# Four column blocks with the sums of B as the stationary side, in a Strassen-like matmul with a row logsumexp

## The chip, the cores and the metric

The kernel runs on one core of a Trainium2 chip. The metric is device time in microseconds (us), the median of several runs. TensorE multiplies a stationary tile of 128x128 (loaded by a weight load) with a moving tile of up to 512 columns and adds the result up in PSUM, which has eight banks of 128x512 f32. VectorE and ScalarE work on 128 rows at a time, GpSimd issues most of the loads, SyncE a few. Each engine works its own queue in order; semaphores tie the queues together.

## The reference

```python
m, k, n = 1024, 4096, 4096
a = randn(m, k); b = randn(k, n)        # float32
x = np.matmul(a, b)
out = logsumexp(x, axis=-1)             # 1024 values
```

The output is one number per row of a: the logarithm of the sum of exponentials over the 4096 columns of that row of the product.

## The kernel before, in words

The products are formed in float16 with float32 sums. A row tile m (there are 8) has 128 rows of a, interleaved: partition p of tile m is row 8p + m. A column block nb (there are 8) has 512 columns of b. The depth of 4096 is 32 slices of 128, taken in 16 pairs.

Apart from block 0 against the first six row tiles, which are plain matmuls (line 227), everything is computed in quarters, in the manner of Winograd's form of Strassen's scheme. A quarter q is two row tiles (2q and 2q+1) against one column block. It is cut in two along rows (the two tiles), depth (the two slices of a pair) and columns (halves of 256), so that four products of halves, c11, c12, c21, c22, are wanted. Instead of eight half-size products there are seven, m1 to m7, on sums of A's halves (s1, s2, s5, and two sums that are put in place in aT) and on sums of B's halves (T1, T4, T6 in the tile tb, and t3 and t7, put in place in the raw block). In the kernel before, A's sums are the stationary side (128x128) and B's sums are the moving side (256 columns). One product is 16 matmuls; a quarter is 112; a block of four quarters is 448. Line 413 issues them all. The order in a quarter is m1 into c11, m5 into c12, m2 into c21, m6 into c22, then m3 on top of c12, m4 on top of c21, m7 on top of c11. In between, ScalarE copies c11 and c12 out after m5 (line 484) and c21 after m2 (line 488), and c12 and c21 again after m3 and m4 (lines 561, 563). m3 writes into c12 only after the copy of line 484, and m7 into c11 likewise. VectorE puts the parts together (lines 498 to 573), takes the maximum of each row (line 89) into a column of the table negmax, and ScalarE takes the exponentials with that maximum as a bias and adds them up into the table tsum (line 94). Those exponentials are put off to the next quarter (the list pending), ahead of which stand that quarter's first copies.

The steps are listed in plan: step 0 is block 1 against quarters 0 to 2, steps 1 to 6 are blocks 2 to 7 against all four quarters, and the last two steps make up block 0 and block 1 against quarter 3. While a block is multiplied, GpSimd loads the next one (line 143) into the eight raw buffers, as soon as those of the block before it are free, and VectorE makes the next block's B sums in the last quarter of a block (the calls of make for t1, t6, t3, t4 and t7 under tail). Each make goes over four groups of four pairs, one instruction of 128x1024 float16 for each group. In step 6, after quarter 1, GpSimd reloads block 1 into the part of aT that is no longer needed (line 595); this load waits for the matmuls of quarter 1.

The order on every engine is the order in which the program emits the instructions (a manual schedule). PSUM tiles go round the eight banks.

At the start, GpSimd builds the identity for the transposes of a (line 295, in masks.py), then issues its loads; VectorE fills zeros, negmax and tsum (lines 294, 296, 297). SyncE brings the first piece of a and of b (lines 308, 313). TensorE does some warm matmuls on zeros (line 291), then transposes pieces of a (line 209) and multiplies them with block 0.

The last quarter (final) merges all columns of negmax and tsum row by row: the smallest of the negated maxima, the exponentials of the differences, the weighted sum, the logarithm (lines 116 to 127 and 515 to 549).

Of the kernel before, what the change touches and what calls it, by code (L numbers as in the profile page):

```python
# [13 lines left out]
def kernel(  # L14
# [6 lines left out]
    nc = tc.nc  # L21
    P = 128
    FD = 512
    H = FD // 2
    f32 = mybir.dt.float32
    f16 = mybir.dt.float16
    AX = mybir.AxisListType
    ALU = mybir.AluOpType
    AF = mybir.ActivationFunctionType
# [4 lines left out]
    MT, KT, NB = M // P, K // P, N // FD  # L34
    MP, KP = MT // 2, KT // 2
    G = 4
    GI = KP // G
# [5 lines left out]
    cst_pool = ctx.enter_context(tc.tile_pool(name="cst", bufs=1))  # L43
    bt_pool = ctx.enter_context(tc.tile_pool(name="btp", bufs=2 * G))
    fix_pool = ctx.enter_context(tc.tile_pool(name="fix", bufs=1))
# [3 lines left out]
    psum_pool = ctx.enter_context(  # L49
        tc.tile_pool(name="psum", bufs=8, space=bass.MemoryType.PSUM)  # L50
    )
# [6 lines left out]
            name=nc.get_next_instruction_name(),  # L58
# [7 lines left out]
    aT = cst_pool.tile([P, KP, 2, MP, 2, P], f16, name="aT")  # L66
    s1 = cst_pool.tile([P, KP, MP, P], f16, name="s1")
    s2 = cst_pool.tile([P, KP, MP, P], f16, name="s2")
    s5 = cst_pool.tile([P, KP, MP, P], f16, name="s5")

    tb = cst_pool.tile([P, 3, KP, H], f16, name="tb")
    stg_slots = tb.rearrange("p t (i j) n -> p (t i) (j n)", j=4)
    NSLOT = 3 * KP // 4
    ident = cst_pool.tile([P, P], f16, name="ident")
    negmax = cst_pool.tile([P, MT, NB + 1], f32, name="negmax")
    tsum = cst_pool.tile([P, MT, NB + 1], f32, name="tsum")

# [4 lines left out]
    def add(o, x, y):  # L82
        nc.vector.tensor_tensor(out=o, in0=x, in1=y, op=ALU.add)  # L83

    def sub(o, x, y):
        nc.vector.tensor_tensor(out=o, in0=x, in1=y, op=ALU.subtract)  # L86
# [44 lines left out]
    class Block:  # L131


        def __init__(self, nb, raw=None, sums=None):
            self.nb = nb
            self.raw = raw or [
                bt_pool.tile([P, GI, 2, FD], f16, name=f"b_{nb}_{g}", tag="bt")
                for g in range(G)
            ]
            self.T1, self.T4, self.T6 = sums or (tb[:, 0], tb[:, 1], tb[:, 2])  # L140

        def load(self, lo, hi):
            nc.gpsimd.dma_start(  # L143
                out=self.raw[lo // GI][:, lo % GI : lo % GI + hi - lo],
                in_=b_rows[:, lo:hi, :, ts(self.nb, FD)],
            )
# [6 lines left out]
        def b(self, i, kp, h):  # L153
            return self.raw[i // GI][:, i % GI, kp, ts(h, H)]

        def make(self, what, lo=None, hi=None):
            if lo is None:
                for g in range(G):
                    self.make(what, g * GI, (g + 1) * GI)
                return  # L160
            u = self.raw[lo // GI][:, lo % GI : lo % GI + hi - lo]
            b11, b12 = u[:, :, 0, 0:H], u[:, :, 0, H:FD]
            b21, b22 = u[:, :, 1, 0:H], u[:, :, 1, H:FD]
            if what == "t1":
                add(self.T1[:, lo:hi], b11, b22)
            elif what == "t6":
                add(self.T6[:, lo:hi], b11, b12)
            elif what == "t4":
                sub(self.T4[:, lo:hi], b21, b11)
            elif what == "t7":  # L170
                add(b21, b21, b22)
            else:
                sub(b12, b12, b22)
# [21 lines left out]
    def load_a(k0, kn, m):  # L195
        slot = stg_slots[:, loads[0] % NSLOT, 0 : kn * P]
        loads[0] += 1
        nc.gpsimd.dma_start(out=slot, in_=a_m[m, :, k0 * P : (k0 + kn) * P])  # L198
        stg[k0, m] = slot
# [55 lines left out]
    arrivals = []  # L255
# [33 lines left out]
    def warm(n):  # L289
        for _ in range(n):  # L290
            nc.tensor.matmul(acc[2][1], zeros[:, 0:P], zeros[:, 0:FD], start=True, stop=True)  # L291

    zeros = s5[:, KP - 1].rearrange("p q c -> p (q c)")
    nc.vector.memset(zeros[:, 0:FD], 0.0)
    make_identity(nc, ident)
    nc.vector.memset(negmax, 3.0e38)
    nc.vector.memset(tsum, 0.0)
    warm(6)

    coming = list(arrivals)  # L300
# [16 lines left out]
    def load(k0, kn, what, x):  # L317
        if len(coming) >= len(arrivals) - 2:
            first(k0, kn, what, x)
        elif what == "a":  # L320
            load_a(k0, kn, x)
        else:
            blk0.load(k0 // 2, k0 // 2 + 1)

    back = []
    for n, (k0, kn, what, x) in enumerate(arrivals):
# [22 lines left out]
    deferred = []  # L349

    def flush():
        for f in pending:
            f()
        pending.clear()
# [5 lines left out]
    again0 = lambda: Block(0, sums=[wide(t[:, :, 0:2]) for t in (s1, s2, s5)])  # L360
    again1 = lambda: Block(1, raw=[wide(aT[:, ts(g, GI), :, 0:2]) for g in range(G)])
    plan = [(lambda: blk1, range(MP - 1))]
    plan += [(lambda nb=nb: Block(nb), range(MP)) for nb in range(2, NB)]
    plan += [(again0, [MP - 1]), (again1, [MP - 1])]

    blk, nxt = None, blk1
    for step, (_, qs) in enumerate(plan):
        blk, nxt = nxt, None
        nb = blk.nb
        more = step + 1 < len(plan)  # L370
        early = more and plan[step + 1][0] is again0
        if more:
            if plan[step + 1][0] is again1:
                nxt = last
            else:
                nxt = plan[step + 1][0]()
                if step == 1:
# [4 lines left out]
                        out=ident[0:1, 0:2], in_=aT[0:1, 0, 0, MP - 1, :, 0]  # L382
# [5 lines left out]
        if step == 0:  # L388

            KH = K // 2  # L390
            for h in range(2):
                a16 = dram_pool.tile([2, P, KH], f16, name=f"a16_{h}")
                for m in range(2):
                    nc.gpsimd.dma_start(out=a16[m], in_=a_m[MT - 2 + m, :, ts(h, KH)])
                for m in range(2):
                    nc.sync.dma_start_transpose(
                        aT[:, ts(h, KP // 2), :, MP - 1, m, :].rearrange("p i t c -> p (i t) c"),
                        a16[m],
                    )
        quads = {}  # L400
        for q in qs:

# [5 lines left out]
            c11, c12 = r0[:, 0:H], r0[:, H:FD]  # L408
            c21, c22 = r1[:, 0:H], r1[:, H:FD]

            def product(c, lhs, rhs, start=False, k=(0, KP)):
                for i in range(*k):
                    nc.tensor.matmul(  # L413
                        c,
                        lhs(i),
                        rhs(i),
                        start=(start and i == 0),
                        stop=(i == KP - 1),
                        skip_group_check=True,
                    )  # L420
# [6 lines left out]
            if final:  # L427
                c22 = psum_pool.tile([P, FD], f32, name="c22", tag="ps")[:, 0:H]


            s = fix_pool.tile([P, 4, H], f32, name=f"s_{step}_{q}", tag="s")
            x, e = s[:, 1::2], s[:, 0:2]
            if final:
                e = fix_pool.tile([P, 2, H], f32, name="e_last", tag="e")
            if joint and q > 0:
                e = e_next
# [78 lines left out]
            if final:  # L515
# [30 lines left out]
                    out=w, in_=w, func=AF.Exp, bias=n0, scale=-1.0, accum_out=l0  # L546
# [44 lines left out]
            if step == 1 and q == 1:  # L591
                a_sums_early(slice(0, KP // 2), MP - 1)
                a_sums_late(slice(0, KP // 2), MP - 1)
            if early and q == 1:
                last = again1().load_all()

    nc.sync.dma_start(out=out.rearrange("(p mt) -> p mt", mt=MT), in_=lg)
# [30 lines left out]
```

## Time and profile before

| What | Number |
|---|---|
| Median of 12 runs | 422.68 us (422.0 to 423.65) |
| Time of the profiled execution | 422.68 us |
| Its span, first to last instruction | 420.4 us |
| Mean granted TensorE clock | 0.999 |
| PE busy | 414.5 us (99%) |
| PE weight loads busy | 349.1 us (83%) |
| DVE (VectorE) busy | 259.0 us (62%), 575 instructions |
| ACT (ScalarE) busy | 109.7 us (26%) |
| POOL (GpSimd) busy | 73.2 us (17%) |
| Moved by DMA | 53.37 MB, mean 127 GB/s |

The profiled execution's own time is 2.3 us above its span, and equals the median of the runs. The busy shares are averages over stages that have different limits. TensorE is called PE, its weight loads PEld, VectorE is DVE, ScalarE ACT, GpSimd POOL and SyncE SP. A group is told by line, engine, operation and what it writes and reads; then come its count, busy time, the mean duration of one in nanoseconds, and the idle time before it with what ended it. In a timeline each line has start, duration, engine, line, operation, and how many instructions were merged into it.

### The profile page before, as it was taken

What the parts mean: (1) busy time and instruction counts of PE and PEld (TensorE: products, weight loads), DVE (VectorE), ACT (ScalarE), POOL (GpSimd) and SP (SyncE); (2) the same over time, 40 slices, a digit from 0 to 9 for tenths busy, and PEclk for the clock granted to TensorE, in tenths of its full rate; (3) what the DMA queues carried; (4) which work ended last, traced back from release to release, by engine and by line L of the source; (5) the groups of instructions that cost most, each with busy time, mean ns of one, the idle gap of its engine ahead of it and who ended that gap; (6) DMA issues with size and microseconds to landing.
All of it is one profiled execution on the core that took longest, in us unless ns stands there. A gap on an engine that the chain in (4) does not pass through costs nothing.

```text
span 420.4 us, 8526 instructions
## 1 busy us (share of the span) xinstructions
PE 414.5 (99%) x3643; PEld 349.1 (83%) x3643; DVE 259.0 (62%) x575; ACT 109.7 (26%) x279; POOL 73.2 (17%) x113
## 2 busy tenths in 40 slices
PE   8999999999999999999999999999999999999996
PEld 2555558888888888888888888888888888888885
DVE  2466687978647783257812694336832587299955
ACT  2222341142132222122222212222221222222124
POOL 7767753001010020003000030000200030020000
PEclk9999999999999999999999999999999999999999
DMA  9999999999999299102990079400990039899000
GB/s 178 204 202 201 202 205 207 207 207 215 189 191 194 48 177 207 18 2 36 207 160 2 2 114 208 82 2 2 179 207 15 2 51 207 144 182 207 14 2 1
DMA packets 57845, 53.37 MB, mean 127 GB/s; under 512 B 10192, under 2 KB 56912, under 8 KB 57808
## 3 DMA queue, kind: packets, MB, share of 16 engines
q0 software_dynamic: 48928, 49.95, 72.0%
q1 hardware_dynamic: 8880, 2.89, 4.1%
q8 instruction: 28, 0.46, 0.4%
q14 instruction: 9, 0.07, 0.0%
HBM read 100.66 MB, written 2.10 MB: 244 GB/s over the span
## 4 chain that ended last, share of the span: by engine, by line
PE 98%; DMA 1%; DVE 0%; ACT 0%; issue 0%; SPq 0%; ACTq 0%
PE acc L413 84%; PE acc L227 10%; PE tps L209 2%; DMA raw_b<-in_b_dram 1%; PE z L413 0%; PE c L413 0%; PE acc L291 0%; DVE aT L220 0%; DVE s L105 0%; ACT s L545 0%; DVE b L314 0%; SPq L308 0%; ACT lg L548 0%; DVE lg L86 0%; DVE nmmin L105 0%
## 5 line engine op out<-in xcount | busy, mean ns | idle before, releaser
L413 PEld LDWEIGHTS <-aT 128*128 128x128 f16 x1856 | 181.6, 98 | 21.1
L413 PEld LDWEIGHTS <-s 128*128 128x128 f16 x1392 | 136.2, 98 | 16.0
L413 PE MATMUL acc<-tb,aT 128*128 128x256 f16 x880 | 108.5, 273 | 0.0
L413 PE MATMUL acc<-b,aT 128*128 128x256 f16 x896 | 106.6, 273 | 0.0
L413 PE MATMUL acc<-b,s 128*128 128x256 f16 x896 | 105.8, 273 | 0.0
L143 POOL DMA_DIRECT2D b<-in_b_dram x51 | 41.1, 816 | 236.6 <-PE acc L413 222.5
L83 DVE TENSOR_TENSOR s<-s 128x256 f32<-128x256 f32 x26 | 11.0, 421 | 77.9 <-ACT s L488 77.9
L413 PE MATMUL acc<-tb,s 128*128 128x256 f16 x448 | 56.9, 273 | 0.0
L86 DVE TENSOR_TENSOR s<-s 128x512 f32<-128x512 f32 (+1 forms) x55 | 30.7, 559 | 38.9 <-ACT s L563 38.0
L484 ACT COPY s<-acc 128x512 f32<-128x512 f32 x26 | 15.2, 585 | 139.3 <-PE acc L413 139.3
L227 PE MATMUL acc<-b,aT 128*128 128x512 f16 x192 | 50.7, 389 | 0.6 <-DVE aT L220 0.4
L94 ACT ACTIVATE acc<-acc,negmax 128x512 f32<-128x512 f32 (+1 forms) x64 | 42.0, 656 | 3.5 <-DVE negmax L89 3.5
L89 DVE TENSOR_REDUCE negmax<-acc 128x1 f32<-128x512 f32 (+1 forms) x64 | 40.4, 671 | 0.6 <-ACT s L523 0.6
L83 DVE TENSOR_TENSOR tb<-b 128x1024 f16<-128x1024 f16 (+1 forms) x64 | 36.1, 616 | 3.5 <-DMA b<-in_b_dram 3.5
L488 ACT COPY s<-acc 128x256 f32<-128x256 f32 x29 | 10.8, 372 | 76.7 <-PE acc L413 72.8
L227 PEld LDWEIGHTS <-aT 128*128 128x128 f16 x192 | 16.8, 99 | 15.1 <-DVE aT L220 1.6
L198 POOL DMA_DIRECT2D tb<-in_a_dram x47 | 25.6, 548 | 5.9 <-issue 1.7
L83 DVE TENSOR_TENSOR acc<-acc,s 128x256 f32<-128x256 f32 x56 | 23.3, 431 | 4.8 <-PE acc L413 0.6
L209 PEld LDWEIGHTS <-tb 128*128 128x128 f16 x192 | 15.0, 100 | 12.5 <-DVE tb L309 1.0
L222 ACT COPY aT<-tps 128x512 f16<-128x512 f16 x24 | 14.0, 585 | 39.1 <-PE tps L209 39.1
L220 DVE COPY aT<-tps 128x512 f16<-128x512 f16 x24 | 10.2, 423 | 19.8 <-PE tps L209 19.8
L83 DVE TENSOR_TENSOR s<-aT 128x256 f16<-128x256 f16 (+1 forms) x78 | 20.2, 313 | 2.2 <-ACT aT L222 2.2
(63 smaller groups left out, 188.0 us busy)
## 6 DMA issues: line engine op xcount, KB each, us to landing
b<-in_b_dram POOLq DMA_DIRECT2D x28, 1024.0 KB, 17.1
tb<-in_a_dram POOLq DMA_DIRECT2D x47, 128.0 KB, 5.9
b<-in_b_dram POOLq DMA_DIRECT2D x8, 512.0 KB, 13.4
aT<-in_b_dram POOLq DMA_DIRECT2D x4, 1024.0 KB, 15.0
b<-in_b_dram POOLq DMA_DIRECT2D x15, 256.0 KB, 6.2
a<-in_a_dram POOLq DMA_DIRECT2D x4, 512.0 KB, 30.0
raw_b<-in_b_dram SPq DMA_DIRECT2D x1, 512.0 KB, 3.9
raw_a<-in_a_dram SPq DMA_DIRECT2D x1, 256.0 KB, 2.8
```

The costliest lines, as they stand in the source:

```text
L83: nc.vector.tensor_tensor(out=o, in0=x, in1=y, op=ALU.add)
L86: nc.vector.tensor_tensor(out=o, in0=x, in1=y, op=ALU.subtract)
L89: nc.vector.tensor_reduce(out=negmax[:, m, nb : nb + 1], in_=pt, axis=AX.X, op=ALU.max, negate=True)
L94: nc.scalar.activation(out=pt, in_=pt, func=AF.Exp, bias=negmax[:, m, nb : nb + 1], scale=scale, accum_out=tsum[:, m, nb : nb + 1],)
L143: nc.gpsimd.dma_start(out=self.raw[lo // GI][:, lo % GI : lo % GI + hi - lo], in_=b_rows[:, lo:hi, :, ts(self.nb, FD)],)
L198: nc.gpsimd.dma_start(out=slot, in_=a_m[m, :, k0 * P : (k0 + kn) * P])
L209: nc.tensor.matmul(pst[:, ts(j, P)], src[:, ts(j, P)], ident, is_transpose=True, start=(j == 0), stop=(j == kn - 1),)
L222: nc.scalar.copy(out=dst, in_=v)
L227: nc.tensor.matmul(pt, aT[:, i, kp, m // 2, m % 2, :], blk0.raw[i // GI][:, i % GI, kp, :], start=(done[m] == 0), stop=(done[m] == KT - 1),)
L413: nc.tensor.matmul(c, lhs(i), rhs(i), start=(start and i == 0), stop=(i == KP - 1), skip_group_check=True,)
L484: nc.scalar.copy(out=e, in_=halves(r0))
L488: nc.scalar.copy(out=s[:, 2], in_=c21)
```

## The change

There are two parts.

At the start, the identity is built behind GpSimd's first load instead of ahead of it, and the fills of negmax and tsum move from VectorE to GpSimd, behind about two dozen of its loads.

For column blocks 3 to 6, the sides of the matmul are exchanged. B's sums, 128 columns at a time, are the stationary side, and A's sums of all four quarters, 512 columns, are the moving side. A block is now two turns, nt = 0 and 1; a turn takes 128 columns of each of the two column halves against all 1024 rows, with seven products of 16 matmuls of 512 columns, and has four PSUM tiles of a whole bank each. What comes out is turned: the columns of x lie on the partitions, and the rows of x along the free axis. So each finished PSUM tile goes through VectorE's transpose of 32x32 blocks into a scratch (two slots in the upper half of T4, and the tile e), a maximum over each block of 32, a subtraction with that row broadcast, an exponential on ScalarE, and a sum over each block of 32. Small tables tnm (in the identity's space) and tts keep the negated maxima and the sums; merge_turned brings the three entries of each into one after every turn. In block 7, after quarter 1, spread_turned copies the tables into columns 3 to 6 of negmax and tsum, with 32 small copies on GpSimd, ahead of the reload of block 1. The copies out of PSUM that ScalarE makes in the other blocks are left to VectorE in a wide turn.

The B sums are made one turn ahead: in turn 0 those of the same block's turn 1, and in turn 1 those of the next block. When the next block is 7, which is not wide, they have the full width, and t4 and t7 are made half before c11 is put together and half after it.

```diff
-    ident = cst_pool.tile([P, P], f16, name="ident")
+    ident_space = cst_pool.tile([P, 3 * P // 2], f16, name="ident")
+    ident = ident_space[:, 0:P]
+    WN = P // 4
+    tnm = ident_space.bitcast(f32).rearrange("p (a c) -> p a c", c=WN)
+    tts = cst_pool.tile([P, 3, WN], f32, name="tts")
+    tmin = cst_pool.tile([P, WN], f32, name="tmin")
...
+            if self.wide:
+                b11, b12, b21, b22 = [t[:, :, ts(nt, P)] for t in (b11, b12, b21, b22)]
...
-    make_identity(nc, ident)
-    nc.vector.memset(negmax, 3.0e38)
-    nc.vector.memset(tsum, 0.0)
     warm(6)
...
+        if len(coming) == len(arrivals) - 3:
+            make_identity(nc, ident)
+        if len(coming) == len(arrivals) - 3 * MT:
+            nc.gpsimd.memset(negmax, 3.0e38)
+            nc.gpsimd.memset(tsum, 0.0)
...
+    WIDE = range(3, NB - 1)
+    slots = tb[:, 1, KP // 2 : KP].rearrange("p i n -> p (i n)").bitcast(f32)
+    slots = [slots[:, 0:FD], slots[:, FD : 2 * FD]]
...
+    def lse_turned(c, slot, h, r):
+        nm = tnm[:, 1 + h, ts(r, WN // 2)]
+        v = blocks32(slot)
+        nc.vector.transpose(out=slot, in_=c)
+        nc.vector.tensor_reduce(out=nm, in_=v, axis=AX.X, op=ALU.max, negate=True)
+        add(v, v, nm.unsqueeze(-1).broadcast_to((P, WN // 2, 32)))
+        nc.scalar.activation(out=slot, in_=slot, func=AF.Exp)
+        return lambda: nc.vector.tensor_reduce(
+            out=tts[:, 1 + h, ts(r, WN // 2)], in_=v, axis=AX.X, op=ALU.add
+        )
+    def merge_turned():
+        nc.vector.tensor_reduce(
+            out=tmin, in_=tnm.rearrange("p a c -> p c a"), axis=AX.X, op=ALU.min
+        )
+        sub(tnm, tnm, tmin.unsqueeze(1).broadcast_to((P, 3, WN)))
+        nc.scalar.activation(out=tnm, in_=tnm, func=AF.Exp, scale=-1.0)
+        nc.vector.tensor_mul(out=tts, in0=tts, in1=tnm)
+        add(tts[:, 0], tts[:, 0], tts[:, 1])
+        add(tts[:, 0], tts[:, 0], tts[:, 2])
+        nc.vector.tensor_copy(out=tnm[:, 0], in_=tmin)
...
+            cols = lambda i, kp, h: blk.b(i, kp, h)[:, ts(nt, P)]
+            product(c11, lambda i: blk.T1[:, i], lambda i: s1[:, i], start=True)
+            product(c12, lambda i: cols(i, 1, 1), lambda i: s5[:, i], start=True)
+            product(c21, lambda i: cols(i, 0, 0), lambda i: s2[:, i], start=True)
+            flush()
+            nc.vector.tensor_copy(out=s[:, 1], in_=c12)
+            add(s[:, 1], s[:, 1], c21)
+            sub(s[:, 0], s[:, 1], c11)
+            for f in deferred:
+                f()
+            deferred.clear()
+            mk("t1")
+            product(c22, lambda i: blk.T6[:, i], lambda i: aT[:, i, 0, :, 1], start=True, stop=True)
+            mk("t6")
+            mk("t3")
+            product(c12, lambda i: cols(i, 0, 1), lambda i: aT[:, i, 0, :, 0], stop=True)
+            sub(s[:, 0], c12, s[:, 0])
+            add(c22, c22, s[:, 0])
+            end12 = lse_turned(c12, slots[0], 1, 0)
+            end22 = lse_turned(c22, slots[1], 1, 1)
+            product(c21, lambda i: blk.T4[:, i], lambda i: aT[:, i, 1, :, 1], stop=True)
+            sub(s[:, 1], c21, s[:, 1])
+            end12()
+            end21 = lse_turned(c21, slots[0], 0, 1)
+            end22()
+            for what in ("t4", "t7"):
+                if last:
+                    for g in range(G // 2):
+                        mk(what, g * GI, (g + 1) * GI)
+                else:
+                    mk(what)
+            product(c11, lambda i: cols(i, 1, 0), lambda i: aT[:, i, 1, :, 0], stop=True)
+            add(c11, c11, s[:, 1])
+            e = fix_pool.tile([P, FD], f32, name=f"ew_{blk.nb}_{nt}", tag="e")
+            end11 = lse_turned(c11, e, 0, 0)
+            end21()
+            if last:
+                for what in ("t4", "t7"):
+                    for g in range(G // 2, G):
+                        mk(what, g * GI, (g + 1) * GI)
+            deferred.extend([end11, merge_turned])
...
+        if blk.wide:
+            wide_step(blk, nxt)
+            continue
+        if step == 1:
+            nc.gpsimd.memset(tnm, 3.0e38)
+            nc.gpsimd.memset(tts, 0.0)
...
             if early and q == 1:
+                spread_turned()
                 last = again1().load_all()
```

Here last (inside wide_step) is true in turn 1 of block 6, and mk makes the B sums of the next turn. The list deferred holds the sum and the merge that a turn leaves to the next one.

## The prediction

> **What bounds it now.** I read the page first: span and the chain that ended last.
>
> ```profile
> span 420.4 us, 8526 instructions
> PE 98%; DMA 1%; DVE 0%; ACT 0%; issue 0%; SPq 0%; ACTq 0%
> ```
>
> TensorE sets the end. The chain in order of time says how:
>
> ```profile
> 58.25 3.45 PE acc L227 x16
> 61.71 347.72 PE acc L413 x3184
> ```
>
> From 61.71 us on there is no gap: 3184 matmuls of 256 columns in 347.72 us, 109.2 ns each. The 16 of 512 columns before them take 215.6 ns each, less than two of 256 (218.4). A block is 448 of these, 48.93 us. So blocks 3 to 6 lie at 147.3 to 343.0 us, and block 7 follows.
>
> Next, how much VectorE does there: the table by stage, for block 6.
>
> ```profile
> 294.10:343.00 48.90, 48.90 (x450) 43.84 (x448) 26.11 (x49) 12.19 (x32) 3.79 (x6) 1.00 0.53 87
> ```
>
> The columns after the stretch are its length, then PE, PEld, DVE, ACT and POOL. VectorE (DVE) is busy 26.1 of 48.9 us. Prices come from the groups with shapes apart:
>
> ```profile
> L83 DVE TENSOR_TENSOR tb<-b 128x512 f16<-128x512 f16 x16 | 6.0, 417 | 2.8 <-DMA b<-in_b_dram 2.8
> L86 DVE TENSOR_TENSOR s<-s 128x512 f32<-128x512 f32 x28 | 19.3, 688 | 38.0 <-ACT s L563 38.0
> L484 ACT COPY s<-acc 128x512 f32<-128x512 f32 x26 | 15.2, 585 | 139.3 <-PE acc L413 139.3
> ```
>
> and, since instructions overlap, from starts in VectorE's timeline:
>
> ```profile
> 184.49 1.28 DVE L89 TENSOR_REDUCE negmax<-acc 128x1 f32<-128x512 f32 x2
> 185.68 2.48 DVE L83 TENSOR_TENSOR tb<-b 128x1024 f16<-128x1024 f16 x4
> 191.53 0.43 DVE L83 TENSOR_TENSOR s<-s 128x256 f32<-128x256 f32 x1 [3.37 <-ACT s L488]
> 192.00 0.42 DVE L86 TENSOR_TENSOR s<-s 128x256 f32<-128x256 f32 x1
> 192.34 2.49 DVE L83 TENSOR_TENSOR tb<-b 128x1024 f16<-128x1024 f16 x4
> 194.75 2.49 DVE L86 TENSOR_TENSOR b<-b 128x1024 f16<-128x1024 f16 x4
> ...
> 411.40 0.21 DVE L86 TENSOR_TENSOR d<-negmax,nmmin 128x48 f32<-128x48 f32 x1
> 411.92 0.21 DVE L124 TENSOR_TENSOR d<-d,tsum 128x48 f32<-128x48 f32 x1 [0.31 <-ACT d L121]
> ```
>
> Two independent 512-column reductions start 0.60 us apart (184.49 to 185.68). Four 1024-column f16 sums take 2.41 us (192.34 to 194.75), 0.60 each, so a 512-column one 0.34 (half the columns save 0.27 us, 417 against 683 ns in duration). An operation that needs the one before it costs 0.13 us more: 0.47 from 191.53 to 192.00, against 0.34 from 192.00 to 192.34. So a 512-column f32 operation is 0.60, or 0.73 when its result is wanted at once. The last two lines are the round trip subtract, exp on ScalarE, multiply: 0.52 us.
>
> [...]
>
> **The change, part by part.** *Start.* GpSimd's first load is issued some 0.7 us earlier (1.44 to 0.74 us) and the identity is ready near 2.0 instead of 1.31; its first use was at 4.02, so that is hidden with 2 us of cover. The earlier load shares the engines with SyncE's two loads, on whose b rows (landing at 5.08) the chain hangs: between +0.3 and -0.3 us, taken as 0. The later fills are two instructions of at most 0.2 us each between loads that run ahead of TensorE: 0, and 0.4 without that cover.
>
> *TensorE, blocks 3 to 6.* 4 x 448 = 1792 matmuls at 109.2 ns (195.7 us) become 896 at 215.7 (193.3 us): -2.4 us. The moving side of four products is now four strips of 128 columns of aT, which the trace does not show; I take no cost, upper bound the whole 2.4. Each block is now two turns (one per 128 columns of each half) of seven products of 3.45 us, 24.16 us a turn, on alternating sets of four PSUM banks.
>
> *VectorE in a turn*, in queue order, measured from the turn's start. Copy c12 (0.73, after product two, 6.90), add c21 (0.73, after product three, 10.35), subtract c11 (0.60); the last sum of the turn before (0.60) and its merge (reduce 0.27, subtract-exp-multiply 0.61 + 0.30, two adds and a copy 0.52: 1.70); t1, t6, t3 for the next turn, 12 x 0.335 = 4.0; subtract and add for c12, c22 (1.34); per quadrant a transpose, maximum, subtraction (0.75 + 0.72 + 0.60 = 2.07) and later a sum (0.60 to 0.72). The f32 transpose is not in the trace. [...] Then t4, t7 (2.7), and for c11 add, transpose, maximum, subtraction and the sum for c21 (3.4). All told 3.4 + 2.0 + 2.3 + 4.0 + 12.2 = 23.9 us, against TensorE's 24.16. So VectorE is 99% full but holds: its tail runs 9.3 us into the next turn, the copy of c12 is done near 10.0 where product five wants it at 13.8, and the add then waits for product three at 10.35, which sets the queue's place anew every turn. The removed ScalarE copies were off the path; ScalarE's four exps (0.65 each) fit.
>
> *Into block 7.* In the last turn of block 6 the sums made are block 7's, at full width: t1, t6, t3 cost 7.2 us instead of 4.0. Counting from product three's end (10.40 with the semaphore): add 0.73, subtract 0.60, sum 0.60, merge 1.70, t1/t6/t3 7.23, subtract and add 1.34, two quadrants 4.14, subtract 0.60, sum 0.72, third quadrant 2.07, sum 0.60, t4 and t7 for two groups 2.42, then for c11 add 0.73, transpose 0.75, maximum 0.72, subtraction 0.69: 25.6 us, ending at 36.0. Behind that ScalarE does the exp of c11 (0.65). Queued behind this exp, in order, is block 7's first copy of c11 and c12 (585 ns), and product m3 of block 7 may not write c12 until it has been read. With semaphores, m3 can start at about 37.4 of the turn, 13.25 of block 7. TensorE gets there after m1, m5, m2, m6: 4 x 1.747 = 7.0. So TensorE stands for 6.25 us. In before, the same copy runs as soon as m5 ends. T4's upper half, delayed behind the scratch slots that lie in it, is ready at 13.2 and 13.8, where m4 now wants it after 15: late by 3.7 us on its own, but covered by the larger wait. Nothing gives the 6.25 us back; TensorE is the bound before and after.
>
> [...]
>
> *Tail.* The 32 small GpSimd copies (nearest row: 178 ns for one of 1x2, so about 6 us) stand ahead of block 1's reload, but they only need the merge, done near 18 us of block 7, and the reload waits for the second quarter's end near 30: 0. If they waited for that quarter's maxima too, the reload would be 9 us late; VectorE's sums would follow, and the last block wants its t1 at 403.7 where they ended at 391.3: still about hidden.
>
> Sum: -2.4 + 6.25 + 2.0 = +5.85. The profiled execution took 422.68 us (span 420.4 and 2.3 around it), which is also the median: 428.5, span 426.2.
>
> **Rivals.** [...] (2) VectorE becomes the bound. Its margin is 0.28 us a turn; a transpose 0.15 dearer adds 0.6 a turn, and the 3.7 us by which product five may be late are used up after some turns. [...] (3) Not slower: the operations that before doesn't show, run at half price. [...] (4) The strips cost TensorE the gain: 430.9. (5) The order holds no such wait, as ScalarE or TensorE would go round it: 420.3. Neither engine does so anywhere in the trace; least likely.
>
> **The numbers.** Main case 0.50 (own range 427.2 to 430), (1) 0.22, (2) 0.15, (3) 0.05, (4) 0.05, (5) 0.03. Measurement tells about 0.2% (0.85 us) from no change. Faster: (5) and a little of (3), 0.04. Same: the rest of (3) and short forms of (1), 0.06. Slower 0.90. The range takes the main case, (1), (4) and the lower part of (2): 425.0 to 432.5.
>
> **What would show it.** Matmuls of 512 columns at about 216 ns in blocks 3 to 6, with no TensorE gap between turns; VectorE 97 to 100% busy there, 23 to 24 us a turn; f32 transposes of 0.71 us; one TensorE gap of about 6 us some 7 us into block 7, before m3, released by ScalarE's copy behind the exp; then matmuls of some 213 ns for a few us. Wrong: gaps within the wide turns (rival 2), no gap at block 7 (5), strips above 216 ns (4), or the reload of block 1 holding the last block.

## The result, and the profile after

The changed kernel takes 428.27 us in the median (427.45 to 428.59, 7 runs), the kernel before 422.63 us (421.8 to 423.65, 29 runs). The ratio of the times is 1.0131, with an interval of 1.0121 to 1.0142: 1.3% slower. The forecast was 428.5. The profiled execution took 428.27 us with a span of 426.5.

First the page after the change: span, the chain that ended last by engine, and the granted TensorE clock in 40 slices of the span.

```profile
span 426.5 us, 6832 instructions
PE 86%; DVE 6%; DMA 5%; POOL 2%; ACT 0%; issue 0%; POOLq 0%; ACTq 0%
PEclk9999999999999999999999999999999996999999
```

TensorE had 98% of the chain before; now VectorE and DMA have a part in it. VectorE's part lies just ahead of the place shown next. DMA's and GpSimd's lie in the first 57 us, where loads of a are waited for; they cost nothing here, since block 1 begins no later than before (61.12 us against 61.71). One digit of the clock, slice 34, is a 6. A slice is 10.66 us, so this is the stretch from 351.9 to 362.5 us.

The chain in order of time, at its last part (start, duration, engine, line):

```profile
351.26 0.70 DVE ew L89
...
352.05 0.63 ACT ew L398
352.68 0.48 ACT s L622
...
353.20 62.28 PE acc L551 x544
```

Read it from below. From 353.20 us TensorE runs to the last block without a gap. What let it begin there is ScalarE's copy of block 7's c11 and c12 (line 622). That copy stood behind the exponential of line 398, which stood behind a subtraction on VectorE (line 89): the chain of the prediction, link by link.

TensorE's timeline at that place, block 7's first quarter (a bracket gives the idle time before and what ended it):

```profile
345.31 1.91 PE L551 MATMUL acc<-tb,aT 128*128 128x256 f16 x16
353.20 3.57 PE L551 MATMUL acc<-b,aT 128*128 128x256 f16 x16 [5.98 <-ACT s L622]
356.56 3.03 PE L551 MATMUL acc<-tb,aT 128*128 128x256 f16 x16
359.43 1.91 PE L551 MATMUL acc<-b,aT 128*128 128x256 f16 x16
```

The first row is m6; m1, m5 and m2 ran before it from 340.06 on. m6 ends at 347.22. Then TensorE stands for 5.98 us. The rows after it are m3, m4 and m7. In the kernel before, m1, m6, m3, m4 and m7 are:

```profile
342.89 1.91 PE L413 MATMUL acc<-tb,s 128*128 128x256 f16 x16
...
348.13 1.91 PE L413 MATMUL acc<-tb,aT 128*128 128x256 f16 x16
349.88 1.91 PE L413 MATMUL acc<-b,aT 128*128 128x256 f16 x16
351.62 1.91 PE L413 MATMUL acc<-tb,aT 128*128 128x256 f16 x16
353.37 1.91 PE L413 MATMUL acc<-b,aT 128*128 128x256 f16 x16
```

m3 and m4 take 6.23 us from start to start now (353.20 to 359.43) and 3.49 before (349.88 to 353.37): 2.74 us for the fallen clock.

The table by stage: the last turn of block 6, the stand, and the stretch after it. After the length come PE, PEld, DVE, ACT and POOL busy with their counts, then the clock, the DMA share and GB/s.

```profile
316.00:340.10 24.10, 24.10 (x114) 10.91 (x112) 22.89 (x45) 1.58 (x4) 2.16 (x3) 1.00 0.02 3
347.22:353.20 5.98, 0.00 (x0) 0.00 (x0) 5.84 (x11) 1.16 (x3) 0.00 (x0) 0.90 1.24 208
353.20:360.00 6.80, 6.80 (x38) 5.06 (x38) 4.40 (x13) 1.14 (x4) 1.60 (x10) 0.59 1.24 207
```

In the turn TensorE has no gap, and VectorE is busy 22.9 of 24.1 us. In the stand VectorE works all the time (5.84 of 5.98). In the last row the clock is 0.59. Read in steps of 0.1 us, it is at half from 352.01 to 358.84 us: over the last 1.2 us of the stand and the first 5.6 us of work.

And the new operations, from the groups with shapes apart (count, busy time, mean ns of one, idle time before):

```profile
L395 DVE STREAM_TRANSPOSE tb<-wide 128x512 f32<-128x512 f32 x24 | 17.0, 710 | 0.3
L89 DVE TENSOR_TENSOR tb<-tb,ident 128x512 f32<-128x512 f32 x24 | 16.6, 692 | 0.8
L396 DVE TENSOR_REDUCE ident<-tb 128x16 f32<-128x512 f32 x24 | 16.5, 686 | 0.9
```

The account between the two profiled executions: the wide blocks run from 146.84 to 340.10 us, 193.3 against 195.7 us of four blocks before, so -2.4. Block 1 begins 0.6 us earlier (61.12 against 61.71), which is scatter of the start, as shown below. By the starts of m1, block 7 begins 2.83 us earlier (340.06 against 342.89; the chain, by which the other two figures are read, puts a product's start up to 0.15 us later). m3 then comes 13.14 us after m1, where it came 6.99 us after it before: +6.15, which is the 5.98 us of idle time and 0.17 for the next product to start up. The clock adds 2.74. From m7 to the last block's z product both take 61.13 us. Together that is +6.06, and z starts just that much later (420.56 against 414.50). The span is longer by 6.1.

### The profile page after: what moved, and what is told of

It is laid out like the page before. It is cut to its first block, busy times and chain, and to the rows that moved or that the text cites. A ratio compares the mean times of both kernels' runs of the same rounds, so it can differ in the third digit from the quotient of the medians.

```text
span 426.5 us, 6832 instructions
## 1 busy us (share of the span) xinstructions
PE 412.9 (97%) x2747; PEld 261.3 (61%) x2747; DVE 338.2 (79%) x773; ACT 83.2 (20%) x191; POOL 79.1 (19%) x149
## 4 chain that ended last, share of the span: by engine, by line
PE 86%; DVE 6%; DMA 5%; POOL 2%; ACT 0%; issue 0%; POOLq 0%; ACTq 0%
PE wide L446 42%; PE acc L551 36%; PE acc L242 6%; DMA tb<-in_a_dram 5%; PE tps L224 2%; DVE tb L89 2%; POOL tb L213 1%; DVE ident L396 1%; DVE b L92 1%; POOL b L156 0%; DVE tb L395 0%; DVE sw L92 0%; DVE tts L399 0%; PE z L551 0%; PE c L551 0%
## 5 line engine op out<-in xcount | busy, mean ns | idle before, releaser
L551 PEld LDWEIGHTS <-aT 128*128 128x128 f16 x832 | 82.8, 100 | 17.0 <-issue 6.2
L446 PEld LDWEIGHTS <-b 128*128 128x128 f16 x512 | 50.1, 98 | 60.4
L551 PEld LDWEIGHTS <-s 128*128 128x128 f16 x624 | 61.1, 98 | 7.5
L446 PE MATMUL wide<-aT,b 128*128 128x512 f16 x256 | 57.9, 379 | 0.0
L446 PE MATMUL wide<-aT,tb 128*128 128x512 f16 x256 | 57.9, 379 | 0.0
L446 PE MATMUL wide<-s,b 128*128 128x512 f16 x256 | 56.6, 379 | 0.0
L551 PE MATMUL acc<-b,aT 128*128 128x256 f16 x384 | 47.2, 279 | 6.0 <-ACT s L622 6.0
L551 PE MATMUL acc<-tb,aT 128*128 128x256 f16 x368 | 48.5, 277 | 0.0
L551 PE MATMUL acc<-b,s 128*128 128x256 f16 x384 | 47.3, 273 | 0.0
L89 DVE TENSOR_TENSOR tb<-b 128x512 f16<-128x512 f16 (+1 forms) x96 | 38.3, 461 | 4.3 <-DMA b<-in_b_dram 4.1
L242 PEld LDWEIGHTS <-aT 128*128 128x128 f16 x192 | 16.6, 98 | 14.2 <-DVE aT L235 1.5
```

The costliest lines, as they stand in the source:

```text
L242: nc.tensor.matmul(pt, aT[:, i, kp, m // 2, m % 2, :], blk0.raw[i // GI][:, i % GI, kp, :], start=(done[m] == 0), stop=(done[m] == KT - 1),)
L446: nc.tensor.matmul(c.rearrange("p (q m) -> p q m", m=P), lhs(i), rhs(i), start=(start and i == 0), stop=(stop and i == KP - 1), skip_group ...
L551: nc.tensor.matmul(c, lhs(i), rhs(i), start=(start and i == 0), stop=(i == KP - 1), skip_group_check=True,)
```

## The experiments

My theory was that of the prediction: a gain of 2.4 us in the wide blocks, lost several times over in one place, where the last wide turn's work on VectorE is too long and ScalarE's queue hands the delay to TensorE. The rivals were that VectorE's load in every turn costs time, that the start does, or that the stand has another cause.

### The two parts apart

The kernel before with the edit of the start alone:

```diff
-    make_identity(nc, ident)
-    nc.vector.memset(negmax, 3.0e38)
-    nc.vector.memset(tsum, 0.0)
     warm(6)
...
+        if len(coming) == len(arrivals) - 3:
+            make_identity(nc, ident)
+        if len(coming) == len(arrivals) - 3 * MT:
+            nc.gpsimd.memset(negmax, 3.0e38)
+            nc.gpsimd.memset(tsum, 0.0)
```

> The kernel before with the start's edit alone (identity behind GpSimd's first load, fills later on GpSimd). Prediction: nothing, 422.6 us. Rival (the 0.6 us by which block 1 began earlier in the changed kernel comes from this edit): 422.0 us, with block 1 again at 61.1 instead of 61.7.

And the changed kernel with the start of the kernel before (the same edit, undone):

> The wide blocks with the start of the kernel before. Theory (the start's edit is worth about 0.4 us, as measured alone, and adds to the rest): 428.7 us. Rival (the start is worth nothing here, since the two parts were measured in different runs): 428.3. Block 1 begins near 61.7 to 62 us.

An unchanged copy of the kernel before was run as well, under a name of its own:

> The kernel before, unchanged, as a kernel of its own. In every run so far the time is 1.79 us above the span, in those of the kernel before 2.24. If the 0.45 us come from what the kernels do (the start's edit or the wide blocks), this run shows 2.24 and 422.5 us. If they come from how the kernel before is run beside the others, it shows 1.79 and 422.1 us, and then the 0.4 us that the start's edit seemed to gain are no gain, since its span was that of before.

The start alone took 421.96 us, ratio 0.999 (0.9981 to 0.9998). The wide blocks alone took 428.13 us, ratio 1.0134 (1.0115 to 1.0152), and stood in the same place for the same time. The waits of TensorE there (us in total, times, longest):

```profile
PE acc L549 <- ACT s L620: 6.0, 1, 6.0
```

So the loss belongs to the wide blocks. The start edit gains about 0.4 us by itself and nothing that can be told from zero beside the wide blocks (428.27 with it, 428.13 without). The 0.4 us does not lie in the span: the start-only runs have a median span of 420.2, the copy of before 420.2 too. It lies between the span and the measured time: 1.79 us there, against 2.22 in the copy of before, 422.41 us (421.57 to 423.48). But the wide blocks with the old start have 1.78 us outside the span as well, so it isn't the start edit as such. What sets these 0.45 us stays open.

The start of block 1 also moves by itself between profiled executions: 61.90 us in the kernel with the old start, 61.12 in the changed one, 61.94 in a later kernel with the new start. So I read nothing out of the 0.6 us of the account.

### VectorE has almost no slack in a turn

Each of the four transposes of a turn is done twice. This adds 32 operations on VectorE that change nothing else.

```diff
-        nc.vector.transpose(out=slot, in_=c)
+        for _ in range(2):
+            nc.vector.transpose(out=slot, in_=c)
```

> [...] Theory (VectorE fills 23.7 of TensorE's 24.16 us in a turn and may lag 3.7 us): 2.8 us more a turn, the lag is used up in the second turn, then TensorE stands some 2.3 us in each of the turns that are left, about 12 us, and block 7's first quarter is later by 6 us more: about 447 us. Rival (VectorE has several us to spare in a turn): 431 us, with only the stand longer.

Measured: 449.48 us, ratio 1.0636 (1.0617 to 1.0654). TensorE's waits, and its timeline at product five of two turns that follow each other:

```profile
PE wide L447 <- DVE sw L462: 12.5, 6, 2.5
PE acc L552 <- ACT s L623: 10.6, 1, 10.6
```

```profile
263.75 3.61 PE L447 MATMUL wide<-aT,b 128*128 128x512 f16 x16 [2.54 <-DVE sw L462]
290.63 5.22 PE L447 MATMUL wide<-aT,b 128*128 128x512 f16 x16 [2.54 <-DVE sw L462]
```

Now VectorE is the bound. A turn takes 26.88 us from start to start (263.75 to 290.63), and the wait is for VectorE's copy of c12 (line 462), which product five overwrites, as the second rival of the prediction has it. In VectorE's timeline a doubled transpose takes 0.75 us more from its start to that of the next instruction (1.49 to 1.50 against 0.74 to 0.75), four of them 3.0. So without them VectorE's need is about 23.9 us a turn, and against TensorE's 24.16 that leaves 0.3 us: the changed kernel holds, but by very little. Its own turns say the same: there the addition of c21 begins 1.09 us after the copy of c12 (252.84 to 253.93), because it waits for TensorE, and 0.79 us after it here (263.02 to 263.81), where it waits for nothing. The stand at block 7 grows from 5.98 to 10.6 us. Four doubled transposes in its chain are 3.0 of the 4.6. The rest comes from VectorE's being behind when that turn begins: against product five its addition of c21 begins 3.3 us later than in the changed kernel, of which the slowed product five gives back 1.7.

The second row shows something else: 2.54 us of pause let the clock fall (the product after it took 5.22 us), while the equal pause in the first row didn't (3.61 us). Of the four pauses of 2.53 or 2.54 us in this execution, two did. The last section comes back to this.

### The stand and the clock

To part the stand from the fall of the clock, 26 matmuls of 512 columns are put between m6 and m3 of block 7's first quarter. They go into a bank that the next quarter will overwrite, and only keep TensorE busy. For this the code takes that quarter's PSUM tiles one quarter earlier.

```diff
+            if early and q == 0:
+                for _ in range(26):
+                    nc.tensor.matmul(quads[1][1], s1[:, 0, 0], wide(s1)[:, 0], start=True, stop=True, skip_group_check=True)
```

> The changed kernel with 26 matmuls of 512 columns put between m6 and m3 of block 7's first quarter, into a bank that the next quarter overwrites; at 0.216 us each they take 5.6 us, which fits the stand of 6.0. Theory (the pause lets the clock fall, and that costs 2.9 us): 425.4 us, with block 7's m3 and m4 at 109 ns per matmul. Rival (the slow matmuls after the stand are not the pause's doing): 428.3 and slow as before.

Measured: 426.76 us (426.07 to 427.25), ratio 1.0097 (1.0074 to 1.012). TensorE's timeline at the stand:

```profile
347.90 5.78 PE L629 MATMUL acc<-s 128*128 128x512 f16 x26
354.06 1.91 PE L551 MATMUL acc<-b,aT 128*128 128x256 f16 x16 [0.38 <-ACT s L622]
355.80 1.91 PE L551 MATMUL acc<-tb,aT 128*128 128x256 f16 x16
358.42 1.91 PE L551 MATMUL acc<-b,aT 128*128 128x256 f16 x16 [0.71 <-ACT s L702]
```

m3 starts when it would have (13.14 us after m1 in both kernels), but m3 and m4 run at full speed, 1.91 us each where they took 3.57 and 3.03: the pause is what lets the clock fall. Yet the time falls by 1.5 us only, not by 2.74; in the two profiles m7 starts 1.87 us sooner after m1 (17.50 against 19.37). With the clock up, m7 is early enough to wait 0.71 us for ScalarE's second copy of c12 (line 702 here, 699 in the changed kernel). m7 writes c11, which lies in the same PSUM tile, and that copy stands behind the exponential of the merge. The slow matmuls had hidden this. It is a wait that the prediction didn't have, and it comes back below.

### What the stand is made of

First, the exponential of c11 in the last turn is put behind block 7's first two copies in ScalarE's queue. All the work stays.

```diff
-            end11 = lse_turned(c11, e, 0, 0)
+            end11 = lse_turned(c11, e, 0, 0, deferred if last else None)
```

Given a list, lse_turned appends its exponential to it instead of emitting it.

> Only ScalarE's exponential of c11 of the last wide turn is moved, behind block 7's first two copies. Theory (ScalarE's queue order makes most of the stand): the copy then waits only for the add that frees its buffer, m3 starts 3.2 us late instead of 6.0, and T4's upper half adds 0.5 us in two pieces, 3.7 us in all. If the clock then stays up, 428.3 - 6.0 + 3.7 - 2.9 = 423.1 us; if it still falls, 426.0. Rival (the stand is set by T4's or VectorE's lateness, not by the exponential in front of the copy): unchanged, 428.3.

Measured: 426.64 us (426.37 to 427.04), ratio 1.0096 (1.0074 to 1.0119). TensorE's timeline:

```profile
350.93 3.57 PE L554 MATMUL acc<-b,aT 128*128 128x256 f16 x16 [3.26 <-ACT s L625]
354.30 3.15 PE L554 MATMUL acc<-tb,aT 128*128 128x256 f16 x16
358.01 1.91 PE L554 MATMUL acc<-b,aT 128*128 128x256 f16 x16 [0.56 <-ACT s L702]
```

The stand shrinks from 5.98 to 3.26 us. So 2.7 us of it come from the order of ScalarE's queue alone: the transpose, maximum and subtraction of c11 on VectorE, plus the exponential, of which block 7 needs nothing. The other 3.3 us are VectorE's work ahead of the addition into c11: the copy's target is the next tile of the one buffer that has the tag s (the pool fix has one of each), and this addition is the last to read the tile before it. The clock fell here too, after 3.26 us; in the four runs the mean clock is 0.992, 0.994, 0.996 and 0.999, so it doesn't always fall, or not for as long.

Next, that work is shortened as well. In the last turn the addition of c11 comes before block 7's t4 and t7, and everything after it (transpose to merge) goes to the end of block 7's first quarter:

```diff
+            if last:
+                end21()
+                mk("t4")
+                mk("t7")
+                leaving.extend([lambda: lse_turned(c11, e, 0, 0)(), merge_turned])
+                continue
...
+            for f in leaving:
+                f()
+            leaving.clear()
```

In the code, the addition stands ahead of the first line shown, and t4 and t7 are no longer made above it.

> In the last wide turn c11 is put together right after its product and before block 7's t4 and t7, and its transpose, maximum, exponential, sum and merge are put off behind block 7's first quarter. Theory (the step from wide to narrow is the whole loss, and the wide blocks themselves gain): TensorE stands at most 0.8 us, no drop of the clock, 428.3 - 6.0 + 0.8 - 2.9 = 420.2 us, which is below before. Rival (the wide blocks cost time themselves, or something else is late behind block 7's first quarter): 424 us or more.

Measured: 422.32 us (421.89 to 423.29), ratio 0.9999 (0.9988 to 1.001). The loss is gone, but 2 us of what I expected are missing. TensorE's waits say where:

```profile
PE acc L551 <- ACT s L699: 1.9, 1, 1.9
PE acc L551 <- ACT s L622: 0.9, 1, 0.9
```

The second is the rest of the stand, which had been reckoned with. The first is m7, on the second copy of c12. This time what holds that copy is VectorE (ScalarE's timeline, then VectorE's):

```profile
353.96 0.37 ACT L699 COPY s<-acc 128x256 f32<-128x256 f32 x1 [4.87 <-DVE s L89]
```

```profile
351.04 2.49 DVE L89 TENSOR_TENSOR b<-b 128x1024 f16<-128x1024 f16 x4
353.45 0.42 DVE L89 TENSOR_TENSOR s<-s 128x256 f32<-128x256 f32 x1
```

The copy goes into a place in s that VectorE's first addition of block 7 (353.45) has to read first, and this addition is queued behind t4 and t7 (the four sums from 351.04 are t7). To try this reading, t7 alone is moved behind that addition:

```diff
-                mk("t7")
+                deferred.append(lambda n=nxt: n.make("t7"))
```

> The kernel of e2_leave_early with one edit: block 7's t7 is made behind the first add and subtraction of its first quarter instead of ahead of them. Theory (m7 waits for ScalarE's second copy of c12, whose target is freed only by that add, which stood behind t7): the gap of 1.86 us before m7 shrinks to about 0.2, m7's groups then wait for t7 0.3 us in all, 422.3 - 1.3 = 421.0 us. Rival (m7 waits for t7 itself or for m4's end): no change, 422.3, or slower, since t7 comes later.

Measured: 421.45 us (420.83 to 422.62), ratio 0.9974 (0.9963 to 0.9986). In the waits the 1.9 us are gone and the 0.9 stay. m7 itself takes 0.5 us longer (351.98 to 354.22), since t7 is now ready later:

```profile
PE acc L551 <- ACT s L622: 0.9, 1, 0.9
```

So the chain at block 7 is: m7, ScalarE's second copy, VectorE's first addition, and whatever VectorE has queued ahead of it.

### Taking the rest away

In the next kernel the last turn adds c11 right after it has subtracted c21. The log-sum-exp work on c21 and c11 and the merge go to the end of block 7's first quarter, t4 is made at once, and t7 behind block 7's first addition.

```diff
+            if last:
+                end12()
+                end22()
+                mk("t4")
+                def leave(c11=c11, c21=c21, c22=c22, e=e):
+                    ends = [lse_turned(c21, c22, 0, 1), lse_turned(c11, e, 0, 0)]
+                    for f in ends:
+                        f()
+                    merge_turned()
+
+                deferred.append(lambda n=nxt: n.make("t7"))
+                leaving.append(leave)
+                continue
```

> In the last wide turn c11 is put together right after c21's subtraction, both lose their transposes and exponentials to the end of block 7's first quarter (c21's into the PSUM tile of c22, which is free then), t4 follows at once, and t7 comes behind the first add of block 7. Theory (all that block 7's first quarter waits for is VectorE's and ScalarE's order at this one place, m7's wait on the second copy of c12 behind that add included): stands of at most 0.3 us in all, 422.3 - 2.7 = 419.6 us, under the kernel before. Rival (something else holds block 7): 421 or more.

Measured: 421.22 us (420.55 to 423.04, 21 runs), ratio 0.9967 (0.9958 to 0.9976). That is a gain over the kernel before, but 1.6 us less than expected. Block 7's first quarter has no gap now. The one that is left is in its second quarter, in TensorE's timeline:

```profile
360.83 1.91 PE L559 MATMUL acc<-b,aT 128*128 128x256 f16 x16 [1.51 <-ACT s L630]
```

It is the same pattern one quarter on. In ScalarE's timeline the merge's exponential, which waits for VectorE, stands ahead of that quarter's first copy:

```profile
360.02 0.28 ACT L409 ACTIVATE ident<-ident 128x96 f32<-128x96 f32 x1 [1.21 <-DVE ident L92]
360.21 0.57 ACT L630 COPY s<-acc 128x512 f32<-128x512 f32 x1
```

So the merge is put behind the second quarter's first copies too:

```diff
-                    merge_turned()
+                    deferred.append(merge_turned)
```

> The kernel of e8_leave_clean with its merge put off once more, behind the first copies and the first add of block 7's second quarter. Theory (the 1.5 us that TensorE stood in that quarter came from ScalarE's exponential of the merge, queued ahead of the copy that m3 waits for): no stand of more than 0.1 us in block 7, 421.2 - 1.5 = 419.7 us, and the span under that of before by about 2.4. Rival (VectorE is now late for something further on): 421 us.

Measured: 427.85 us (426.99 to 428.67), ratio 1.0127 (1.0107 to 1.0146). This was a clear miss. The second quarter is clean as intended, but TensorE waits in the last quarter of block 7, and the clock falls again (m7 took 3.36 us from start to start):

```profile
393.35 3.57 PE L559 MATMUL acc<-b,aT 128*128 128x256 f16 x16 [5.76 <-ACT s L707]
396.71 2.62 PE L559 MATMUL acc<-s 128*128 128x256 f16 x16
```

It is m7's wait again. VectorE's addition is late because VectorE waits for the reload of block 1 (VectorE's timeline):

```profile
391.81 0.69 DVE L89 TENSOR_TENSOR tb<-aT 128x1024 f16<-128x1024 f16 x1 [4.38 <-DMA aT<-in_b_dram]
392.42 0.42 DVE L89 TENSOR_TENSOR s<-s 128x256 f32<-128x256 f32 x1
```

And the reload is late because of GpSimd's small copies ahead of it (GpSimd's timeline, a part of it):

```profile
366.44 0.19 POOL L420 COPY tsum<-tts 32x8 f32<-32x8 f32 x1
366.67 0.56 POOL L420 COPY negmax<-ident 32x8 f32<-32x8 f32 x1
367.17 0.66 POOL L420 COPY tsum<-tts 32x8 f32<-32x8 f32 x1
...
373.81 3.50 POOL L156 DMA_DIRECT2D aT<-in_b_dram  x4
```

The copies begin only 1.3 us later than in the kernel before this one (362.55 us against 361.28). But after the 20th, VectorE begins eight float16 sums, then four more (VectorE's timeline):

```profile
366.46 4.94 DVE L89 TENSOR_TENSOR s<-b 128x1024 f16<-128x1024 f16 x8
```

Each of the last 12 copies takes 0.56 to 0.67 us, about three times as long, while those beside VectorE's two reductions just before (from 365.26 us) took 0.19 us. One of the first 20 was as slow (0.68 us at 363.64), beside a subtraction of 128x512 float32 on VectorE (363.58). The reload is issued at 373.81 us, 9.1 us after the end of quarter 1's matmuls (364.72), where it was at 367.58 in the kernel before this one. No run tries the copies beside other work of VectorE on purpose, so this cause rests on what coincides in the trace; that the copies made the reload late is tested next.

The copies are only needed at the very end. So in the last kernel the reload is issued ahead of them:

```diff
-                spread_turned()
                 last = again1().load_all()
+                spread_turned()
```

> The kernel in which the merge comes later, with one thing moved: GpSimd issues the reload of block 1's tiles ahead of its 32 small copies instead of behind them. Theory (the reload was late only because the copies ahead of it were slowed while VectorE adds from SBUF; the copies themselves are needed only by the last merge, near 410 us, and at 0.6 us each they take 19 us, so they have time): block 7 runs without a gap, the reload is issued by about 363 us, TensorE keeps its full clock, 419.7 us, the span about 2.4 us under that of the kernel before. Rival (VectorE is late in block 7 for another reason, or the copies, now beside more of VectorE's sums, cost VectorE time): a wait of TensorE in block 7 remains and the time is 421 us or more, with a span within 1.5 us of the kernel before or above it.

Measured: 419.81 us (419.24 to 420.41, 5 runs) against 422.28 (421.8 to 423.07, 9 runs) of before beside it, ratio 0.9935 (0.9921 to 0.9948). GpSimd's timeline, and TensorE's part of the chain that ended last:

```profile
365.20 3.50 POOL L156 DMA_DIRECT2D aT<-in_b_dram  x4 [22.94 <-PE acc L559]
368.66 0.53 POOL L420 COPY negmax<-ident 32x8 f32<-32x8 f32 x1
...
381.62 0.67 POOL L420 COPY tsum<-tts 32x8 f32<-32x8 f32 x1
```

```profile
61.94 85.72 PE acc L559 x784
147.66 193.38 PE wide L448 x896
341.05 19.21 PE acc L559 x176
360.28 47.32 PE acc L559 x432
```

The reload waits for nothing but TensorE (the end of quarter 1's matmuls). The copies are slow (13.6 us for all 32) and nobody waits for them. From 61.94 us on TensorE has no wait above 0.2 us, so the gain of the wide blocks (193.38 us where four blocks took 195.7) is kept. The median span is 418.0 against 420.0 beside it. So 2.0 us come from within the span and the rest, about 0.45, from outside it.

This version beats both kernels: by 0.65% the one before, which ran beside it, and by about 2% the changed one, which ran at another time.

## Why the prediction was right

*TensorE in blocks 3 to 6, -2.4 us.* Right: 193.3 us against 195.7. The strips on the moving side cost nothing, so the fourth rival falls.

*VectorE in a turn, 23.9 us, holding with 0.28 to spare.* Right: 23.9 from the doubled transposes, with 0.3 to spare. The working's 0.75 us for a transpose and the 0.71 of the prediction's last line were estimates of mine that no run showed: the trace of before has no f32 transpose. In the changed kernel one takes 710 ns, and 0.74 to 0.75 us from its start to that of the next instruction. The second rival describes the kernel that has four more transposes, not this one: at 0.75 us more per quadrant it gave stalls of 2.5 us a turn and a stand of 10.6. A margin of 0.3 us is all that keeps the changed kernel from it.

*The stand at block 7, 6.25 us, m3 at 13.25 of the block.* Right: 5.98 us, m3 at 13.14 (353.20 less 340.06), behind the copy and exponential named. The experiment on the order of the exponential removed 2.7 us of it, and the one that also puts c11's addition ahead of t4 and t7 left 0.9. So the cause is shown, and not only the place. One wait was missing in the working, though it cost nothing in the changed kernel: see the clock. The third and fifth rivals fall: no new operation went at half price (710, 692 and 686 ns, where 512 f32 columns took 688 before), and no engine went round the wait.

*The clock, +2.0 us in the sum.* The clock fell, as forecast, but the size was too small. No run shows the 2.0 us, which was an estimate of mine for work at half rate behind the stand; the changed kernel lost 2.74 us, with 5.6 us of work at half rate. The 16 matmuls of m3 took 210 ns each (3.36 us), where the last line of the prediction has some 213, an estimate too. Keeping the clock up gave back only 1.5, because m7 then waits for a copy. This wait was in the kernel and not in my working: I looked at ScalarE's first copy of block 7 and not at the second, which stands behind the merge's exponential and, when that isn't late, behind VectorE's first addition. So (1), a clock that stays up in the stand (2.0 us under the forecast, 426.5), is false, for the clock fell. That the kernel with the clock kept up came near that number (426.76) is chance: by the clock alone it would have been 428.27 less 2.74, or 425.5, and m7's wait makes up most of the rest (0.87 us in the profile).

*Start, 0.* Right for the span and for the changed kernel. The gain of 0.4 us that the edit shows alone lies outside the span, of which the working said nothing.

*Tail, 0.* Right for the changed kernel: its reload was issued at 372.85 us, released by TensorE, 8.4 us after the last of the small copies. The aside was wrong, though. It had a reload that comes 9 us late "still about hidden". In the kernel with the later merge it came 9.1 us after quarter 1's end, and TensorE stood 5.76 us. I had counted when the last block wants its t1, and not what is queued behind the sums on VectorE while they wait. (The eight sums that need the reload also end at 392.1 us in the trace of before, not at 391.3.)

That the sum came so near, 428.5 against 428.27, is partly luck, since errors of under a microsecond went both ways. The clock was 0.74 too short. Against that the stand was up to 0.27 too long, the profiled execution's start happened to be 0.6 earlier, and the working kept the 2.3 us of before outside the span, where the changed kernel has 1.79. The span alone was forecast at 426.2 and came out at 426.5.

## What to carry to other kernels

Where a kernel goes from one way of working to another, follow each engine's queue across the seam: the last step of the old way leaves work that the new one doesn't need, but stands behind. Put the parts of it that free a buffer first and everything else, an exponential or a merge, behind the next step's first copies; and issue a load ahead of small copies that nobody waits for. A gain of 0.6% on the bounding engine is kept only if no queue hands it a wait, so look at all the copies it waits for, the second as well as the first.

## What the runs showed of the hardware

The TensorE clock fell behind some pauses of TensorE and not behind others. Here are those of 1.5 us and more from block 3 to the last product for which a timeline was read, with the product of 16 matmuls behind each, from its start to that of the next product. Without a pause that takes 1.74 to 1.75 us for 256 columns and 3.45 for 512.

| Kernel | Pause (us) | Length | Columns | Product behind it |
|---|---|---|---|---|
| log-sum-exp put off | 359.32 to 360.83 | 1.51 | 256 | 1.75 |
| c11 before t4 and t7 | 352.52 to 354.38 | 1.86 | 256 | 1.74 |
| transposes doubled | 234.34 to 236.88 | 2.54 | 512 | 3.45 |
| the same | 261.21 to 263.75 | 2.54 | 512 | 3.45 |
| the same | 288.09 to 290.63 | 2.54 | 512 | 5.05 |
| the same | 341.83 to 344.36 | 2.53 | 512 | 5.14 |
| the same | 363.55 to 374.16 | 10.61 | 256 | 3.37 |
| exponential behind | 347.67 to 350.93 | 3.26 | 256 | 3.37 |
| merge later | 387.59 to 393.35 | 5.76 | 256 | 3.36 |
| changed | 347.22 to 353.20 | 5.98 | 256 | 3.36 |

So the product was slow behind each pause of 3.26 us and more and at full speed behind those of 1.51 and 1.86. Of the four of 2.53 or 2.54 us in one execution, two were followed by a slow product and two were not: there the length of the pause alone didn't decide, and what else does was not shown. The mean granted clock of that execution is 0.977, that of the kernel before 0.999. In the changed kernel the clock fell 4.79 us after the pause began and was at half for 6.83 us (352.01 to 358.84), which cost 2.74 us; behind the pauses of 2.54 and 2.53 us that slowed it, the product was 1.60 and 1.69 us longer. With the old start, the chain's last 544 matmuls in one piece take 62.40 us behind the stand of 6.0, where the changed kernel has 62.28; at 109.2 ns each they would take 59.4. These are single traces, and the ends of matmuls in them are modelled. The start of a kernel may differ: in the last kernel's profiled execution the granted clock reads 8 tenths in the first of the 40 slices (10.5 us), where the changed kernel has 9.

In the changed kernel 31 of GpSimd's 32 copies of 32x8 float32 took 0.19 or 0.20 us. In the kernel with the later merge they took 0.56 to 0.67 us beside VectorE's float16 sums, and single ones took 0.66 us (the one left in the changed kernel, at 360.15) and 0.68 us (later merge, at 363.64) beside a subtraction of 128x512 float32.

About 0.45 us of the measured time lies outside the span in the kernel before and not in any kernel with an edit of the start or of the wide blocks. It stays with the kernel when it is run under another name, and its cause was not found.
